# Scan of a Mamba-2 layer: two weightings written as scaled activations on ScalarE instead of GpSimd tensor products

## Chip, core and metric
One core of a Trainium2 chip runs the whole layer as one program. The metric is device time in microseconds (us), the median of the runs. The engines are named as the profile names them: PE (TensorE, matmul), DVE (VectorE), ACT (ScalarE), POOL (GpSimd), SP (SyncE, which here only issues DMAs).

## The reference, cut to what matters
```python
mod = (sc @ ada_w[i] + ada_b[i]).reshape(-1, 6, D_MODEL)      # sc = silu(c), D_MODEL = 1024
...
acum = jnp.cumsum(ac, axis=-1)                                # ac = dt * a, chunks of 128 tokens
scores = jnp.einsum("bclhn,bcshn->bhcls", ch, bh) * segsum_exp(ac)
y_diag = jnp.einsum("bclhs,bcshp->bclhp", scores, xdt)        # xdt = xs * dt
...
y_off = jnp.einsum("bclhn,bchpn,bhcl->bclhp", ch, states[:, :-1], jnp.exp(acum))
```
The modulation is a row vector (1024) times a matrix (1024 x 6144). The scan runs over 8 chunks of 128 tokens with 8 heads, forwards and backwards, with time steps `dt` for each token, head and direction. After it come an output projection, a selection of experts and their evaluation, which take most of the time and are not touched.

## The kernel before
The work around the change has three stretches. The **projection** (about 77 to 355 us) multiplies the tokens with 21 weight blocks on PE, with convolutions on DVE. The **backward loop** (about 355 to 433 us) has 12 steps `n` over `pre`: four for the context tokens, then the chunks 7 to 0. The **forward loop** (about 433 to 541 us) goes over the chunks 0 to 7. Each engine works through its own queue in the order in which the code issues instructions; SP issues the DMAs in such a queue too.

The modulation is computed in 24 slices beside the other work. A slice is a 512 KB block of `ada_w`, loaded by `ask()` (L293) into the tile `ld`, of which there are two buffers. `modulation()` multiplies it with `sc` (L320), one factor for each partition and each of 8 groups of 128 columns; DVE sums the 8 groups (L322, L323, L325), PE sums over partitions (L304). `beside()` runs a piece of this at the end of each loop step: first the sums of one slice, then the multiplication of the next. Six slices are multiplied in the projection, 12 in the backward loop, six in the forward loop.

`spread(z)` of the scan makes for a chunk the two tiles `pf` and `pb` (128 x 8 x 128): a triangular mask times `dt`, one factor for each partition and head (L648). `decays(z)` multiplies them on PE (L693, L694), ACT takes the exponent into `em` (L696), and DVE works on it.

Also in the loops are the key products `step_keys` (PE L356, into the one PSUM buffer `pk`; ACT copies it out into `h2T`, L358; after every second one SP stores it to `m_dram`, L360, and loads the next `wqT` block, L342). A backward step holds one key product, a forward step of the chunks 0 to 4 holds four. `reach` puts `dtx` on ACT (L625), from which PE and then ACT make `de` (L632); `natural` copies `xn` and `bn` out of PSUM on ACT (L592, L596); `weigh` (`xw`, L602) and the product with `dcol` (L598) are on POOL.

Of the kernel before, what the change touches and what calls it, by code (L numbers as in the profile page):

```python
# [13 lines left out]
AF = mybir.ActivationFunctionType  # L14
OP = mybir.AluOpType
# [3 lines left out]
P = 128  # L19
D = 1024  # L20
KD = D // P
# [8 lines left out]
NH = 8  # L30
# [42 lines left out]
def layer_kernel(ctx, tc, A, dbg=None):  # L73
    nc = tc.nc
# [32 lines left out]
    sc = glob.tile([P, KD, 2], F32, name="sc")  # L107
# [19 lines left out]
    dt = mixp.tile([P, NZ, 16], F32, name="dt")  # L127
# [168 lines left out]
    def modulation():  # L296

        nc.sync.dma_start(gater, A["ada_b"][2048:3072].partition_broadcast(P))
        last = []

        def spread(j, wa):
            row, k = j // KD, j % KD
            pr = prs[:, j % 4]
            nc.tensor.matmul(pr, ones, wa, start=True, stop=True)  # L304
            if row == 0:
                g = gater[:, k * P:(k + 1) * P]
                nc.vector.tensor_tensor(g, pr, g, op=OP.add)
            else:
                nc.vector.scalar_tensor_tensor(wa, pr, 1.0, ident, op0=OP.mult, op1=OP.mult,
                                               accum_out=(b2c if row == 1 else s2c)[:, k:k + 1])  # L310

        prs = psL.tile([P, 4, P], F32, name="pc")
        for j in range(24):
            while j not in ready:
                yield -1
            while last and last[0][0] < call[0]:
                spread(*last.pop(0)[1:])
                yield 0.25
            w = ready[j]
            nc.gpsimd.tensor_tensor(w, w, sc[:, :, 0:1].to_broadcast([P, KD, P]), op=OP.mult)  # L320
            yield -1
            nc.vector.tensor_tensor(w[:, :4], w[:, :4], w[:, 4:], op=OP.add)  # L322
            nc.vector.tensor_tensor(w[:, :2], w[:, :2], w[:, 2:4], op=OP.add)  # L323
            wa = lpr.tile([P, P], F32, name="wa", bufs=3)
            nc.vector.tensor_tensor(wa, w[:, 0], w[:, 1], op=OP.add)  # L325
            del ready[j]
            last.append((call[0], j, wa))
            yield 1.1
        yield -1
        while last:  # L330
            spread(*last.pop(0)[1:])
        nc.vector.tensor_tensor(b2c, b2c, adab[:, 24:32], op=OP.add)
        nc.vector.tensor_tensor(s2c, s2c, adab[:, 32:40], op=OP.add)
        nc.vector.tensor_scalar(s2c, s2c, 1.0, None, op0=OP.add)
        nc.vector.tensor_tensor(s2c, s2c, n2c, op=OP.mult)
        yield 1.0
# [30 lines left out]
    with ExitStack() as st:  # L367
# [123 lines left out]

        held = {}
        later.append(modulation())
        for n, c in enumerate(order):

# [80 lines left out]
    with ExitStack() as st:  # L576
# [67 lines left out]
        def spread(z):  # L644
            pf = s2p.tile([P, NH, P], F32, name="pf")
            pb = s2p.tile([P, NH, P], F32, name="pb", bufs=1)
            for d, (buf, half) in enumerate(((pf, upper), (pb, lower))):
                nc.gpsimd.tensor_tensor(buf, half[:, None].to_broadcast([P, NH, P]),  # L648
                                        dt[:, z, d * 8:d * 8 + 8, None].to_broadcast([P, NH, P]), op=OP.mult)
            C[z] = pf, pb  # L650

        pre = [(NT, 0), (NT + 1, 1), (NT + 1, 0), (NT, 1)] + [(z, 1) for z in range(NT - 1, -1, -1)]
# [6 lines left out]
        for n, (z, d) in enumerate(pre):  # L659
            nxt, far = None, iter(())  # L660
            if n + 1 < len(pre):
                zn = pre[n + 1][0]
                if zn in todo:
                    todo.remove(zn)
                    far = reach(zn, 1)
                    next(far)
                    natural(zn)
                if zn:
                    nxt = weigh(*pre[n + 1])
                if n == len(pre) - 4:  # L670
                    spread(0)
            step_keys(1)
            if z < NT:
                carried(z, 1, hs[1])
            if z:
                hs[d] = state(z, d, hs[d], xw)
            next(far, None)
            xw = nxt
            if n == 2:
                dbg("hf", hs[0])  # L680
            if n == 3:
                dbg("hb", hs[1])
            for q in range(2 * n, min(16, 2 * n + 2)):
                nc.vector.tensor_scalar(ltA[:, q], gt_s if q < 8 else lt_s, an[:, q:q + 1], None, op0=OP.mult)
            ask()
            beside(2.2)
# [928 lines left out]
```

## Time and profile before
| | us |
|---|---|
| median of 3 runs | 3078.5 |
| lowest and highest | 3078.39, 3080.2 |
| the profiled execution, its own time | 3079.81 |
| its span in the trace | 3078.1 |

Over the span PE is busy 92%, DVE 85%, POOL 44% and ACT 34%. These are averages over stretches with different limits; the scan has to be read by its own rows. In a row, busy time is followed by a count (x...), "idle before" names what ended a wait, and times in a timeline count from the span's start.

### The profile page before, as it was taken

What the parts mean: (1) busy time and instruction counts of PE and PEld (TensorE: products, weight loads), DVE (VectorE), ACT (ScalarE), POOL (GpSimd) and SP (SyncE); (2) the same over time, 40 slices, a digit from 0 to 9 for tenths busy, and PEclk for the clock granted to TensorE, in tenths of its full rate; (3) what the DMA queues carried; (4) which work ended last, traced back from release to release, by engine and by line L of the source; (5) the groups of instructions that cost most, each with busy time, mean ns of one, the idle gap of its engine ahead of it and who ended that gap; (6) DMA issues with size and microseconds to landing.
All of it is one profiled execution on the core that took longest, in us unless ns stands there. A gap on an engine that the chain in (4) does not pass through costs nothing.

```text
span 3078.1 us, 41667 instructions
## 1 busy us (share of the span) xinstructions
PE 2824.7 (92%) x14905; PEld 2374.3 (77%) x14905; DVE 2624.8 (85%) x5164; ACT 1061.4 (34%) x2026; POOL 1350.1 (44%) x1059
## 2 busy tenths in 40 slices
PE   7999878898888886999999999999999999999996
PEld 3777667664555556898888997998998898998894
DVE  4898788558999998889988888888988888888886
ACT  3224332332677664232322222222222322222222
POOL 0212455420000001666566666556666566666650
PEclk8999999899999987999999999999999999999998
DMA  6111346241212225898989998999998999999982
GB/s 212 61 35 48 100 141 192 83 160 56 117 66 103 110 110 190 303 315 312 314 307 329 336 345 316 325 350 324 335 338 315 327 344 325 338 330 334 321 314 108
DMA packets 334544, 722.66 MB, mean 235 GB/s; under 512 B 24560, under 2 KB 167168, under 8 KB 333056
## 3 DMA queue, kind: packets, MB, share of 16 engines
q0 software_dynamic: 112176, 408.47, 37.3%
q1 hardware_dynamic: 222160, 311.53, 28.9%
q8 instruction: 117, 1.92, 0.2%
q14 instruction: 91, 0.75, 0.1%
HBM read 658.56 MB, written 61.35 MB: 234 GB/s over the span
## 4 chain that ended last, share of the span: by engine, by line
PE 51%; DVE 30%; DMA 8%; issue 6%; POOL 4%; ACT 2%; SPq 0%; DVEq 0%; POOLq 0%; ACTq 0%
PE pa L990 22%; PE pv L1428 7%; PE pv L1429 7%; PE pv L1427 7%; DMA gr<-in_peer_u_dram,idx 4%; DVE o L1211 3%; DVE cfm L408 3%; PE pa L68 3%; DMA gr<-in_peer_v_dram,idx 2%; DVE oh L1083 2%; DVE ob L1203 2%; DVE gr L1299 2%; DVE oh L1081 2%; POOL gr L1276 2%; PE po L68 1%
## 5 line engine op out<-in xcount | busy, mean ns | idle before, releaser
L1276 POOL DMA_INDIRECT gr<-in_peer_u_dram,idx x384 | 524.8, 1367 | 370.3 <-DVE gr L1299 271.9
L1276 POOL DMA_INDIRECT gr<-in_peer_v_dram,idx x384 | 543.5, 1415 | 326.1 <-DVE h2T L1311 233.1
L1311 DVE SCALAR_TENSOR_TENSOR h2T<-gr,wv,h2T 128x1024 f32<-128x1024 f32 x381 | 488.5, 1282 | 47.5 <-DMA gr<-in_peer_v_dram,idx 41.1
L1428 PE MATMUL pv<-vl,wh 128*128 128x512 f32 x1240 | 496.0, 400 | 30.5 <-DVE vl L61 30.3
L1299 DVE SCALAR_TENSOR_TENSOR gr<-gr,h2T 128x1024 f32<-128x1024 f32 x384 | 458.1, 1221 | 51.0 <-DMA gr<-in_peer_u_dram,idx 50.3
L1427 PE MATMUL pv<-vh,wl 128*128 128x512 f32 x1240 | 493.4, 398 | 5.1 <-ACT vh L60 5.1
L1429 PE MATMUL pv<-vh,wh 128*128 128x512 f32 x1240 | 493.6, 398 | 0.0
L60 ACT ACTIVATE vh<-v 128x512 fp32r<-128x512 f32 x256 | 161.3, 632 | 666.6 <-PE pv L1429 636.3
L990 PE MATMUL pa<-hh,ul 128*128 128x320 f32 x2000 | 334.1, 309 | 0.7 <-DVE ul L982 0.7
L990 PE MATMUL pa<-hl,uh 128*128 128x320 f32 x2000 | 334.1, 309 | 0.3 <-ACT ga L1390 0.3
L990 PE MATMUL pa<-hh,uh 128*128 128x320 f32 x2000 | 334.0, 309 | 0.0
L990 PEld LDWEIGHTS pa<-hl,uh 128*128 128x128 f32 x2000 | 304.8, 188 | 3.5 <-ACT ga L1390 0.8
L1428 PEld LDWEIGHTS pv<-vl,wh 128*128 128x128 f32 x1240 | 236.3, 191 | 91.8 <-DVE vl L61 38.3
L990 PEld LDWEIGHTS pa<-hh,ul 128*128 128x128 f32 x2000 | 303.5, 188 | 1.2 <-DVE ul L982 1.2
L990 PEld LDWEIGHTS pa<-hh,uh 128*128 128x128 f32 x2000 | 303.6, 188 | 0.0
L1390 ACT ACTIVATE ga<-pa 128x320 f32<-128x320 f32 x252 | 109.6, 437 | 508.4 <-PE pa L990 507.4
L1427 PEld LDWEIGHTS pv<-vh,wl 128*128 128x128 f32 x1240 | 236.3, 191 | 60.7 <-ACT vh L60 6.4
L1429 PEld LDWEIGHTS pv<-vh,wh 128*128 128x128 f32 x1240 | 236.4, 191 | 54.5
L1189 PEld LDWEIGHTS pg<-o,o 128*128 128x128 f32 x1280 | 175.4, 208 | 126.8 <-ACT o L1206 106.6
L1189 PE MATMUL pg<-o,o 128*128 128x128 f32 x1280 | 189.5, 298 | 74.0 <-ACT o L1206 64.5
L61 DVE TENSOR_TENSOR vl<-v,vh 128x512 fp32r<-128x512 f32 x256 | 176.2, 689 | 95.1 <-ACT vh L60 94.7
L1206 ACT ACTIVATE o<-ob,tr 128x128 f32<-128x128 bf16 x640 | 209.3, 398 | 96.3 <-DVE ob L1203 94.3
(344 smaller groups left out, 4292.8 us busy)
## 6 DMA issues: line engine op xcount, KB each, us to landing
v<-in_peer_v_dram SPq DMA_DIRECT2D x256, 256.0 KB
u<-in_peer_ut_dram SPq DMA_DIRECT2D x87, 512.0 KB
g_dram<-stg SPq DMA_DIRECT2D x10, 4096.0 KB
gm<-g_dram SPq DMA_DIRECT2D x64, 640.0 KB
h2T<-in_peer_ut_dram SPq DMA_DIRECT2D x41, 512.0 KB
ld<-in_ada_w_dram SPq DMA_DIRECT2D x24, 512.0 KB
w<-in_w_in_t_dram SPq DMA_DIRECT2D x21, 512.0 KB
raw<-in_ada_w_dram SPq DMA_DIRECT2D x8, 1024.0 KB
```

Of the source, the lines that this page charges most:

```text
L60: nc.scalar.activation(hi, src, AF.Copy)
L61: (eng or nc.vector).tensor_tensor(lo, src, hi.bitcast(F32), op=OP.subtract)
L68: nc.tensor.matmul(out, a(k)[i], b(k)[j], start=start and t == 0 and k == 0, stop=stop and t == 2 and k == n - 1)
L990: nc.tensor.matmul(pa[half], x[:, k], y[:, k, half * TH:half * TH + TH], start=t == 0 and k == 0, stop=t == 2 and k == KD - 1)
L1189: nc.tensor.matmul(pg[:, j], o2[:, j], o1[:, j], start=True, stop=True)
L1206: nc.scalar.activation(o2[:, j], ob[:, :, j], AF.Copy, scale=tr[:, 1, t4 * 4 + j:t4 * 4 + j + 1])
L1276: nc.gpsimd.indirect_dma_start(out=g, out_offset=None, in_=A[t], in_offset=bass.IndirectOffsetOnAxis(ap=idx[:, b, e:e + 1], axis=0))
L1299: nc.vector.scalar_tensor_tensor(g, g, 1.0, h2, op0=OP.mult, op1=OP.mult, accum_out=act[:, e:e + 1])
L1311: nc.vector.scalar_tensor_tensor(ac, g, wv[:, e:e + 1], ac, op0=OP.mult, op1=OP.add)
L1427: nc.tensor.matmul(Out.pv[t], wl[:, sl], self.vh, start=i == 0, stop=False)
L1428: nc.tensor.matmul(Out.pv[t], wh[:, sl], self.vl, start=False, stop=False)
L1429: nc.tensor.matmul(Out.pv[t], wh[:, sl], self.vh, start=False, stop=i == GE - 1)
```

## The change
The multiplication of a slice, one GpSimd tensor product over 128 x 1024, becomes eight ScalarE activations (Copy with a scale for each partition) over 128 x 128, in place. `spread` becomes 16 such activations instead of two GpSimd products. Nothing else is edited.
```diff
             w = ready[j]
-            nc.gpsimd.tensor_tensor(w, w, sc[:, :, 0:1].to_broadcast([P, KD, P]), op=OP.mult)
+            for k in range(KD):
+                nc.scalar.activation(w[:, k], w[:, k], AF.Copy, scale=sc[:, k, 0:1])
             yield -1
...
             for d, (buf, half) in enumerate(((pf, upper), (pb, lower))):
-                nc.gpsimd.tensor_tensor(buf, half[:, None].to_broadcast([P, NH, P]),
-                                        dt[:, z, d * 8:d * 8 + 8, None].to_broadcast([P, NH, P]), op=OP.mult)
+                for h in range(NH):
+                    nc.scalar.activation(buf[:, h], half, AF.Copy, scale=dt[:, z, d * 8 + h:d * 8 + h + 1])
             C[z] = pf, pb
```
The lines behind the first place move down by one in the changed kernel, so that L358 there is L359, and so on.

ACT's queue in the forward loop, from the exponent `em` of one chunk to that of the next, before (names in brackets are the semaphores that an instruction waits for; DMAHW is a DMA's):
```order
L696 ACTIVATE em<-psg 128x1024 [waits PE_49]
L358 ACTIVATE h2T<-pk 128x512 [waits DMAHW0_49,PE_49]
L358 ACTIVATE h2T<-pk 128x512 [waits PE_49]
L632 ACTIVATE de<-ps 128x512 [waits DVE_49,PE_49]
L358 ACTIVATE h2T<-pk 128x512 [waits DMAHW4_49,PE_49]
L358 ACTIVATE h2T<-pk 128x512 [waits PE_49]
L625 ACTIVATE dtx<-dta 128x512 [waits Activation_49]
L696 ACTIVATE em<-psg 128x1024 [waits DVE_49,PE_49]
```
The same place in the changed kernel:
```order
L697 ACTIVATE em<-psg 128x1024 [waits PE_49]
L359 ACTIVATE h2T<-pk 128x512 [waits DMAHW0_49,PE_49]
L359 ACTIVATE h2T<-pk 128x512 [waits PE_49]
L633 ACTIVATE de<-ps 128x512 [waits PE_49]
L359 ACTIVATE h2T<-pk 128x512 [waits DMAHW4_49,PE_49]
L650 ACTIVATE pf<-tri,dt 128x128 [waits DVE_49]
L650 ACTIVATE pf<-tri,dt 128x128 x7
L650 ACTIVATE pb<-tri,dt 128x128 [waits DVE_49]
L650 ACTIVATE pb<-tri,dt 128x128 x7
L359 ACTIVATE h2T<-pk 128x512 [waits PE_49]
L321 ACTIVATE ld<-ld,sc 128x128 [waits DMAHW2_49]
L321 ACTIVATE ld<-ld,sc 128x128 x7
```
Twenty-four instructions have come in between: the 16 of `spread` ahead of the step's last `h2T`, and the eight of the slice behind it, the first of which waits for the slice's DMA. `dtx` and the next `em` (L626, L697) follow them.

ACT's queue in a backward step, before (from `dtx` to the `dtx` of the step after):
```order
L625 ACTIVATE dtx<-dta 128x512 [waits Activation_49]
L592 ACTIVATE xn_2338<-pdg 128x512 [waits PE_49]
L596 ACTIVATE bn_2339<-pcb 128x256 [waits PE_49]
L358 ACTIVATE h2T<-pk 128x512 [waits DMAHW4_49,PE_49]
L632 ACTIVATE de<-psg 128x512 [waits DVE_49,PE_49]
```
The same step in the changed kernel:
```order
L626 ACTIVATE dtx<-dta 128x512 [waits Activation_49]
L593 ACTIVATE xn_2415<-pdg 128x512 [waits PE_49]
L597 ACTIVATE bn_2416<-pcb 128x256 [waits PE_49]
L359 ACTIVATE h2T<-pk 128x512 [waits DMAHW4_49,PE_49]
L633 ACTIVATE de<-psg 128x512 [waits DVE_49,PE_49]
L321 ACTIVATE ld<-ld,sc 128x128 [waits DMAHW3_49,DVE_49,Activation_49]
L321 ACTIVATE ld<-ld,sc 128x128 x7
```
Here the slice stands behind `de` and ahead of the next step's `dtx`.

SP's queue in the changed kernel, around the load of the slice that the first forward step multiplies (DMAHW2, as in the ACT rows):
```order
L361 DMA m_dram<-h2T 128x8x128 [waits DMAHW6_49,DMAHW0_49,Activation_49]
L343 DMA h2T<-in_wqT_dram 128x1024 [waits DMAHW7_49]
L344 DMA sk<-in_skT_dram 128x128 [waits DMAHW1_49,PE_49]
L361 DMA m_dram<-h2T 128x8x128 [waits DMAHW4_49,Activation_49]
L293 DMA ld<-in_ada_w_dram 128x8x128 [waits DMAHW2_49,DVE_49]
```
The order of SP's DMAs is the one of before; the load (L293) stands behind a store that waits for ACT, and that ACT instruction is the step's last `h2T` (L359).

## Rows read from the trace of the kernel before
**Rows 1.** Windows of the backward and forward loop: busy time by engine, clock, DMA share.
```profile
355.00:433.00 78.00, 54.76 (x378) 49.30 (x377) 69.45 (x105) 25.79 (x49) 46.54 (x32) 0.96 0.55 168
433.00:541.00 108.00, 88.42 (x725) 81.59 (x723) 85.86 (x108) 28.50 (x44) 54.51 (x28) 0.91 0.56 172
```
**Rows 2.** The lines L320 and L648: durations min/median/max in ns; waits.
```profile
L320 POOL TENSOR_TENSOR ld<-ld,sc x24: 1902/1906/3152, 90.9 to 525.7; 128x1024 f32<-128x1024 f32 x24
...
DMA ld<-in_ada_w_dram: 64.9, 15
...
L648 POOL TENSOR_TENSOR pf<-tri,dt x8: 1891/1898/2871, 408.6 to 516.7; 128x1024 f32<-128x1024 f32 x8
...
PE psg L694: 8.3, 6
```
**Rows 3.** Timeline of DVE and POOL, forward loop: start, us, what.
```profile
453.61 0.69 DVE L617 TENSOR_TENSOR htmp<-h,tot 128x512 f32<-128x512 f32 x1
466.87 2.38 DVE L617 TENSOR_TENSOR htmp<-h,tot 128x512 f32<-128x512 f32 x1
...
466.35 2.34 POOL L648 TENSOR_TENSOR pb<-tri,dt 128x1024 f32<-128x1024 f32 x1
```
**Rows 4.** Timeline of ACT, later stage: four activations with a scale per partition.
```profile
880.86 1.30 ACT L1206 ACTIVATE o<-ob,tr 128x128 f32<-128x128 bf16 x4
```
**Rows 5.** Timeline of ACT, backward loop.
```profile
373.61 0.62 ACT L625 ACTIVATE dtx<-dta 128x512 f32<-128x512 f32 x1
...
374.87 0.61 ACT L358 ACTIVATE h2T<-pk 128x512 f32<-128x512 f32 x1
...
386.06 0.62 ACT L625 ACTIVATE dtx<-dta 128x512 f32<-128x512 f32 x1
...
400.49 0.62 ACT L625 ACTIVATE dtx<-dta 128x512 f32<-128x512 f32 x1
```
**Rows 6.** Timeline of SP and POOL, backward loop: a slice's issue and multiplication.
```profile
386.84 0.38 SPq L293 DMA_DIRECT2D ld<-in_ada_w_dram  x1
...
390.76 1.90 POOL L320 TENSOR_TENSOR ld<-ld,sc 128x1024 f32<-128x1024 f32 x1 [3.08 <-DMA ld<-in_ada_w_dram]
...
430.25 1.90 POOL L320 TENSOR_TENSOR ld<-ld,sc 128x1024 f32<-128x1024 f32 x1 [5.03 <-DMA ld<-in_ada_w_dram]
```
**Rows 7.** Timeline of ACT, forward loop.
```profile
433.07 1.03 ACT L696 ACTIVATE em<-psg 128x1024 f32<-128x1024 f32 x1 [5.95 <-PE psg L694]
...
447.04 1.02 ACT L696 ACTIVATE em<-psg 128x1024 f32<-128x1024 f32 x1 [10.62 <-PE psg L694]
...
458.82 1.02 ACT L696 ACTIVATE em<-psg 128x1024 f32<-128x1024 f32 x1 [2.68 <-PE psg L694]
459.74 0.59 ACT L358 ACTIVATE h2T<-pk 128x512 f32<-128x512 f32 x1
...
464.95 0.60 ACT L358 ACTIVATE h2T<-pk 128x512 f32<-128x512 f32 x1 [1.19 <-PE pk L356]
466.80 0.60 ACT L358 ACTIVATE h2T<-pk 128x512 f32<-128x512 f32 x1 [1.25 <-PE pk L356]
467.29 0.62 ACT L625 ACTIVATE dtx<-dta 128x512 f32<-128x512 f32 x1
...
526.45 1.02 ACT L696 ACTIVATE em<-psg 128x1024 f32<-128x1024 f32 x1 [11.40 <-PE psg L694]
```
**Rows 8.** Timeline of SP, POOL and PE in the same forward step.
```profile
467.42 0.38 SPq L360 DMA_DIRECT2D m_dram<-h2T  x1
467.90 0.52 SPq L293 DMA_DIRECT2D ld<-in_ada_w_dram  x1
...
473.34 1.90 POOL L320 TENSOR_TENSOR ld<-ld,sc 128x1024 f32<-128x1024 f32 x1 [4.65 <-DMA ld<-in_ada_w_dram]
...
461.07 1.16 PE L356 MATMUL pk<-sk,h2T 128*128 128x128 f32 x8
```
**Rows 9.** Windows at the first forward step, columns as in rows 1.
```profile
440.00:442.00 2.00, 0.85 (x4) 0.85 (x5) 0.67 (x1) 0.00 (x0) 2.00 (x2) 0.50 0.34 123
442.00:444.00 2.00, 2.00 (x11) 2.00 (x11) 0.00 (x0) 0.00 (x0) 1.96 (x2) 0.50 0.00 0
446.00:448.00 2.00, 2.00 (x21) 2.00 (x20) 1.11 (x1) 0.96 (x2) 0.00 (x0) 1.00 0.04 8
```

## The prediction
> **What bounds the kernel now.** I went from the page's chain of waits, where PE and DVE carry most of the span, to the windows of the stretches that the change touches. In the backward loop DVE is busy 69.45 of 78 us and PE 54.76; in the forward loop PE 88.42 of 108 and DVE 85.86; ACT has only 25.79 and 28.50 [rows 1]. So the engine that gets the work looks empty, and the engines it may relieve look full. What decides is therefore not ACT's busy share but where in its queue the new instructions stand, and what they wait for. For that I read the lines L320 and L648 with their waits, and then the timelines of ACT, SP, POOL and PE over single loop steps.
>
> The view of the lines says that POOL's 24 slice products take 1.91 us each and that 15 of them came after 64.9 us of waiting for the slice's DMA; the products of `spread` take 1.9 us or more each, and PE waited 8.3 us for them at L694 [rows 2]. The first is the important one: POOL stands still for slices, and today little stands behind it.
>
> The timelines also show DVE and POOL in each other's way. The same DVE product takes 0.69 us alone and 2.38 us when it starts 0.52 us after a POOL product of 2.34 us [rows 3].
>
> **The change part by part.** *Removed:* 24 slice products and 16 spread products on POOL, 24 x 1.91 + 16 x 1.90 = 76 us by the medians [rows 2], and DVE's stretching beside them. The sum of DVE's stretching is worth nothing where another engine sets the step; its size is weighed under the rivals.
>
> *The price of one new activation* is not in the trace for this shape and these types. The nearest row has four activations over 128 x 128 with a per-partition scale in 1.30 us [rows 4]: taking 0.40 for the last and 0.30 from start to start for the three others, 0.30 x 3 + 0.40 = 1.30. A slice of eight is then 7 x 0.30 + 0.40 = 2.5 us and holds the next instruction up by 2.4; a spread of 16 holds it up by 4.8. These stand on ACT, in order. If the pitch were 0.35, a step with both would cost 24 x 0.05 = 1.2 us more.
>
> *Projection.* Six slices, 6 x 2.4 = 14 us of ACT, lie beside PE's matmuls, whose evictions have three PSUM buffers. I price this at 0. If the cover is gone, it is the last two slices, ahead of two evictions that feed DVE: up to 2 x 2.4 = 5 us. On the other side DVE has some 2 us of stretching less. Bounds -2 and +5.
>
> *Backward loop.* A slice's load is issued when DVE has summed the one before it, and lands 390.76 - 386.84 = 3.9 us later [rows 6]. Behind the slice ACT now holds `dtx`, `xn`, `bn`, `h2T` and `de` of the next step; from `dtx`'s start to `h2T`'s end they take 374.87 + 0.61 - 373.61 = 1.9 us back to back [rows 5], with `de` 2.4. In every second step SP has a store of `m_dram` ahead of the load, and that store waits for `h2T`. There the loop is: slice ends, 1.9 to the end of `h2T`, 0.5 for SP's store, 5.4 to the landing (the forward price below), 2.5 for the next slice: 10.3 us. In the step after it the load goes out earlier, in the shade of this, so: 2.4 + 2.4 = 4.8. A pair is 15.1, where two steps now take 400.49 - 386.06 = 14.4 [rows 5]: +0.7 for each of some four pairs, +3. The spread of chunk 0 stands in ACT's queue too, 4.8, where its POOL version cost about 3 more in its step: +2. The last slice is waited for once more and its 2.5 and the `dtx` behind it precede the first `em`, which today follows 433.07 - 432.15 = 0.9 after POOL's slice at 430.25 ends [rows 6, 7]: +3.5. So the first `em` is some 9 us late. From there to the second `em` the rows have 447.04 - 433.07 = 14.0 [rows 7], lengthened by POOL's spread and a half clock; on ACT it is about 0.9 + 1.0 for `de` and `h2T`, 2.8 until the first `pb` piece, 5 for PE's decay products: 10. The second `em` is late by 9 - 4 = 5, bounds -5 and +10.
>
> *Forward loop,* the main term. Five steps (chunks 0 to 4) have this queue on ACT: `em`, `h2T`, `h2T`, `de`, `h2T`, 16 of spread, `h2T`, eight of the slice, `dtx`, `em`. The load of the slice stands in SP's queue behind the store that waits for the last `h2T`; in the trace that store is issued at 467.42, as `h2T` of 466.80 ends, the load at 467.90, and POOL starts at 473.34 [rows 7, 8]. So a slice cannot be there before 0.02 + 0.48 + 5.44 = 5.9 us after that `h2T` ends. POOL bears this wait today with little behind it. ACT will stand in it with the next chunk's `dtx`, `em` and `h2T`, and PE's second key product needs the one PSUM buffer that this `h2T` empties. The queued cycle, from the start of that key product (461.07 [rows 8]):
> to the third `h2T` 464.95 - 461.07 = 3.9 [rows 7, 8]; its pitch 0.5; spread 4.8; the last `h2T` 0.6; store, load and landing 5.9; slice 2.4; `dtx` 0.5 (467.29 - 466.80 shows such a pitch); `em` 459.74 - 458.82 = 0.9; `h2T` 0.6 and 0.05 to PE [rows 7]. Sum 20.2 us.
> Within it PE can run ahead by its decay products, one key product and the products of the chunk before, then has nothing for about 7 us. Where PE had been busy only 0.85 of 2 us, the clock stood at 0.50 (1.2 GHz); it still did in the next 2 us, all busy, and was at 1.00 (2.4 GHz) from 446 to 448 [rows 9]. I add 2 us, half of the 3.9 at the low level: 22.2. Bounds 18.7 (a landing in 3.9 and no clock loss) and 25 (all 3.9 doubled, 1.2 for pitch).
> The last interval, chunk 5, has no key products; I take 13 (ACT's chain with one more wait for a slice; bounds 11 and 18). Now the six intervals take 526.45 - 447.04 = 79.4 [rows 7]. After: 5 x 22.2 + 13 = 124. That is +45, bounds 5 x 18.7 + 11 = 104.5, +25, and 5 x 25 + 18 = 143, +64.
>
> *Sum:* 0 + 5 + 45 = +50. Behind the scan nothing takes it back: the output projection begins with `y` of the last chunk. The profiled execution took 3079.81, 1.7 over its span and 1.3 over the median; on the median the forecast is 3078.5 + 50 = **3128**. Corners of all bounds at once (+18 and +79) are rarer than one; for this case I take +26 to +66.
>
> **A rule beside the rows.** A row pair shows DVE waiting out a POOL product, 1.7 us in one instruction [rows 3]. The Trainium skill, GPSIMD Engine Reference, section 1 (Specifications), says that GpSimd's SBUF interfaces are shared with VectorE and contend with its instructions with two SBUF inputs; the pair agrees. By the rule alone DVE's steps get shorter and the time falls, as in the first rival below; by the queues it rises.
>
> **The rivals.**
> *Faster: DVE and POOL are untangled and ACT's waits hide.* For it: the stretched DVE row [rows 3], DVE's 69.45 of 78 [rows 1], ACT's idle share. Then the forward steps fall to PE's own 458.82 - 447.04 = 11.8, 6 x 11.8 = 71 instead of 79.4, -9; the first interval falls by 2; the backward steps fall from 7.2 to some 6, -10: 3078.5 - 21 = 3057. It decides if the slice has landed when ACT comes to it, and if ACT's own 14.3 us a step (20.2 - 5.9) hid as well; I see nothing that would. Chance 0.05.
> *ACT's work counts, the wait for the slice does not.* If loads ran a step ahead, the forward cycle would be 14.3: 5 x 14.3 + 13 = 84.5, +5, and with the backward loop about +8: 3086. Against it: the store and the load in SP's queue [rows 8]. Chance 0.08.
> *PE's clock stays low through the scan.* Each forward cycle then pays the upper bound, and the backward steps some 1 to 2 more: 5 x 25 + 13 = 138, +59, and +15: 3152. For it: the windows at 0.50 [rows 9]; against: PE still works 11.8 of 22 us. Chance 0.08.
> *Nothing:* the scan's delay is absorbed and 3078 stays. PE waits for nothing but this chain there. Chance 0.03.
>
> **How the numbers follow.** My case has 0.76 and the time 3128, its own range 3104 to 3144. The range to hold 8 in 10 takes in the second rival and part of the clock rival: 3084 to 3150. A measurement of this kernel can tell about 0.2%, 6 us, from no change. Faster holds the first rival and a little of mine gone wrong, 0.06; the same 0.04; slower 0.90.
>
> **What would show it.** In the changed profile: L321 on ACT in eights of about 2.5 us, with some 6 us of idle time ahead of each in the forward loop, ended by the DMA of `ld`; intervals of 20 to 24 us between `em` rows; PE waiting for ACT at the key products (L357); DVE's L618 at 0.7 us nearly everywhere and the scan still longer, by 40 to 55 us; the stretches before 355 us and behind the scan unchanged. I would be wrong if the load were issued ahead of the store, if the slice landed much sooner than 5.4 us after its issue, or if the activations had another pitch than 0.30.

## The result, and the profile after

The changed kernel takes 3144.43 us (median of four runs, 3140.9 to 3157.01); the kernel before, run beside it, 3079.35 (3078.39 to 3085.02). The ratio is 1.0218, 95% interval 1.0202 to 1.0235: 65 us slower. The forecast was 3128 (3084 to 3150). The profiled execution took 3140.9 us, with a span of 3139.1.

The scan has all of it. Its eight exponents `em` serve as a clock below: the first is at 456.89 us (before 433.07), the second at 469.46 (447.04), the last at 591.27 (526.45). So the backward side costs 23.8 us, the first interval gives 1.4 back, and the rest of the forward loop costs 42.4. The load of `nw`, the first behind the scan, is issued at 603.01 instead of 540.40, which is 62.6 later, and the profiled execution takes 61.1 us more than the one before: the stretches behind the scan give back only a few us.

Windows of the loops, columns as in [rows 1]. The stretches are the same times of the span; the work in them is less, since the loops last longer.
```profile
355.00:433.00 78.00, 51.83 (x290) 47.05 (x289) 42.70 (x89) 46.21 (x127) 17.93 (x17) 0.80 0.42 122
433.00:541.00 108.00, 73.05 (x530) 68.78 (x529) 47.03 (x73) 59.21 (x161) 7.75 (x7) 0.83 0.43 125
```
ACT, the engine that got the work, is busy 59.21 of 108 us; DVE has fallen to 47.03 and PE to 73.05. No engine is full. That is how a chain of waits looks, and the view of waits from 355 to 610 us names it (us in total, times, longest):
```profile
ACT ld L321 <- DMA ld<-in_ada_w_dram: 63.4, 13, 6.3
...
PE pk L357 <- ACT h2T L359: 33.0, 6, 7.2
...
PE psg L630 <- ACT dtx L626: 19.6, 4, 5.6
```
ACT stands for slices, and PE stands for what is queued behind them. POOL did the same before [rows 2], with less in its queue (what stood there shows in e8). The lines of the two new groups over the whole span (count, then busy us and mean ns, then idle time ahead and its releasers):
```profile
L321 ACT ACTIVATE ld<-ld,sc 128x128 f32<-128x128 f32 x192 | 58.6, 388 | 71.9 <-DMA ld<-in_ada_w_dram 71.6 <-DVE ld L323 0.3
...
L650 ACT ACTIVATE pb<-tri,dt 128x128 f32<-128x128 f32 x64 | 19.5, 390 | 0.0
```
One forward step on ACT, from `em` to `em` (compare [rows 7]):
```profile
489.99 1.00 ACT L697 ACTIVATE em<-psg 128x1024 f32<-128x1024 f32 x1
490.89 0.58 ACT L359 ACTIVATE h2T<-pk 128x512 f32<-128x512 f32 x1
493.64 0.60 ACT L359 ACTIVATE h2T<-pk 128x512 f32<-128x512 f32 x1 [2.17 <-PE pk L357]
495.07 0.60 ACT L633 ACTIVATE de<-ps 128x512 f32<-128x512 f32 x1 [0.84 <-PE ps L630]
496.86 0.60 ACT L359 ACTIVATE h2T<-pk 128x512 f32<-128x512 f32 x1 [1.19 <-PE pk L357]
497.35 2.44 ACT L650 ACTIVATE pf<-tri,dt 128x128 f32<-128x128 f32 x8
499.69 2.43 ACT L650 ACTIVATE pb<-tri,dt 128x128 f32<-128x128 f32 x8
502.03 0.58 ACT L359 ACTIVATE h2T<-pk 128x512 f32<-128x512 f32 x1
508.42 2.44 ACT L321 ACTIVATE ld<-ld,sc 128x128 f32<-128x128 f32 x8 [5.82 <-DMA ld<-in_ada_w_dram]
510.77 0.61 ACT L626 ACTIVATE dtx<-dta 128x512 f32<-128x512 f32 x1
511.29 1.00 ACT L697 ACTIVATE em<-psg 128x1024 f32<-128x1024 f32 x1
```
and on SP (the rows of before are in [rows 8]):
```profile
502.63 0.38 SPq L361 DMA_DIRECT2D m_dram<-h2T  x1
503.10 0.53 SPq L293 DMA_DIRECT2D ld<-in_ada_w_dram  x1
```
The last `h2T` ends at 502.61; 0.02 later the store goes out, 0.47 later the slice's load, and 5.32 later ACT can start on the slice. PE in the same step:
```profile
491.52 2.08 PE L357 MATMUL pk<-sk,h2T 128*128 128x128 f32 x8 [6.68 <-ACT h2T L359]
493.39 1.64 PE L630 MATMUL ps<-tri,dtx 128*128 128x128 f32 x8
494.87 1.06 PE L640 MATMUL ps<-CT,h 128*128 128x128 f32 x8
...
503.36 0.39 PE L695 MATMUL psg<-pb,ltA 128*128 128x128 f32 x2
```
PE had finished the input of `em` soon after 503.36; `em` ran at 511.29, because it stands behind the slice. An engine that takes its queue in order cannot step over an instruction whose data are late. (The Trainium skill, Perfetto Trace Analysis, section "Tensor Engine Instruction (MATMUL, LD_WEIGHTS)", calls ACT, DVE and GpSimd strict FIFO; these rows agree.)

### The profile page after: what moved, and what is told of

Read it like the earlier page. It is cut to its first block, busy times and chain, and to the rows that moved or that the text cites. A ratio compares the mean times of both kernels' runs of the same rounds, so it can differ in the third digit from the quotient of the medians.

```text
span 3139.1 us, 41947 instructions
## 1 busy us (share of the span) xinstructions
PE 2842.5 (91%) x14905; PEld 2394.4 (76%) x14905; DVE 2582.1 (82%) x5164; ACT 1151.2 (37%) x2346; POOL 1260.6 (40%) x1019
## 4 chain that ended last, share of the span: by engine, by line
PE 47%; DVE 31%; DMA 8%; issue 5%; ACT 5%; POOL 3%; SPq 1%; DVEq 0%; POOLq 0%; ACTq 0%
PE pa L991 19%; PE pv L1429 7%; PE pv L1430 7%; PE pv L1428 7%; DVE o L1212 3%; DVE cfm L409 3%; DMA gr<-in_peer_u_dram,idx 3%; DVE gr L1300 2%; DMA ld<-in_ada_w_dram 2%; POOL gr L1277 2%; DVE oh L1084 2%; DVE ob L1204 2%; DVE cfm L411 2%; DVE oh L1082 2%; DVE ef L1070 1%
```

## The experiments

Theory (queue): ACT stands in the slice's transfer, with `dtx`, `em` and `h2T` behind it. Rival 1 (work): what costs is the time of the activations themselves. Rival 2 (clock): what costs is PE's lower clock. The table has the exponents' times from each profile, the mean of the five intervals from the second exponent to the seventh ("step"), the median, and the ratio to the kernel before on the same chip (whose median was 3081.57 for e1 to e4, 3079.11 for e5 to e8 and 3077.49 for e9).

| | first `em` | second | last | step | median | ratio, interval |
|---|---|---|---|---|---|---|
| before | 433.07 | 447.04 | 526.45 | 12.9 | 3079.35 | |
| changed | 456.89 | 469.46 | 591.27 | 21.8 | 3144.43 | 1.0218 (1.0202 to 1.0235) |
| e1 spread only | 430.43 | 440.98 | 529.97 | 14.5 | 3081.97 | 0.9999 (0.9982 to 1.0015) |
| e2 slices only | 454.72 | 463.87 | 571.34 | 19.0 | 3125.37 | 1.0136 (1.0112 to 1.016) |
| e3 changed, early load | 433.76 | 446.56 | 529.55 | 14.7 | 3080.92 | 1.0003 (0.9989 to 1.0018) |
| e4 e1, early load | 430.44 | 441.23 | 524.48 | 14.8 | 3079.57 | 0.9997 (0.998 to 1.0013) |
| e5 one piece of eight | 435.31 | 447.23 | 538.80 | 15.8 | 3098.04 | 1.0065 (1.0042 to 1.0089) |
| e6 load ahead of one store | 433.46 | 446.30 | 536.88 | 14.5 | 3092.87 | 1.0045 (1.0031 to 1.006) |
| e7 before, early load | 433.85 | 447.43 | 515.96 | 12.1 | 3075.63 | 0.9976 (0.9962 to 0.9989) |
| e8 loops' slices, early load | 429.22 | 435.48 | 503.49 | 12.0 | 3055.78 | 0.9915 (0.9893 to 0.9937) |
| e9 all slices, early load | 433.03 | 440.91 | 508.02 | 11.8 | 3061.22 | 0.9949 (0.9933 to 0.9964) |

**e1: only `spread` on ACT.** The kernel before with the second hunk of the change.

> Only spread is on ScalarE (16 activations a chunk), the slices stay on GpSimd as before. Queue theory (the lost time is ScalarE standing in the slice's DMA wait): nothing on ScalarE waits for a transfer, its own work in a forward step is 0.9 + 4 x 0.6 + 0.6 + 4.8 + 0.5 = 9.2 us, under the steps of before; 3065 to 3090. Work theory (the activations' own time is what costs): 4.8 of the 7.2 us that each of five forward steps got are still there, so about two thirds of the forward loop's 42 us, 3105 to 3115. Clock theory (PE's lower clock is most of it): the clock in the forward loop returns to about 0.91 only if the steps do.

The time is that of before. The work rival falls as the cause of the 65 us: two thirds of the forward loop's added work are there and 65 us are not. But the step is not shorter than before either, 14.5 against 12.9.

**e2: only the slices on ACT.** The kernel before with the first hunk.

> Only the slices are on ScalarE, spread stays on GpSimd. Queue theory: the forward cycle loses 4.8 us of spread and keeps the wait, 20.3 measured mean - 4.8 = 16 to 17.5 us, 12 to 20 us over before for the loop, and the backward loop's +22 stays: 3110 to 3130. Work theory: only 2.4 of 7.2 us a forward step remain, 14 us in the forward loop and some 20 in the backward loop by their own time of 12 x 2.4 = 29 less cover: about 3095 to 3105, with the intervals between exponents under 15 us.

3125.37, inside the queue theory's range; the first exponent is 21.7 late, nearly as in the changed kernel. The step, 19.0, is longer than the 16 to 17.5 expected. ACT in the step from 500.85 to 519.47:
```profile
507.65 0.60 ACT L359 ACTIVATE h2T<-pk 128x512 f32<-128x512 f32 x1 [1.19 <-PE pk L357]
509.50 0.60 ACT L359 ACTIVATE h2T<-pk 128x512 f32<-128x512 f32 x1 [1.25 <-PE pk L357]
516.60 2.45 ACT L321 ACTIVATE ld<-ld,sc 128x128 f32<-128x128 f32 x8 [6.50 <-DMA ld<-in_ada_w_dram]
```
The last `h2T` comes 1.85 after the third, held by PE's key product; with `spread` between them it came 502.03 - 496.86 = 5.2 after. So leaving `spread` out shortens the chain by 3.3, not 4.8, and the slice's wait is longer.

**e3: the changed kernel, its load a step earlier.** No instruction is added; `ask()` goes to the step's start. It does the same in the backward loop.
```diff
         for z in range(NT):
+            ask()
             more = z + 1 < NT
...
             step_keys(1)
-            ask()
             beside(2.2)
```

> The changed kernel, with the slice's load issued at the start of a loop step instead of its end, so that it has a step's time to land and stands ahead of the store in SP's queue. No instruction is added or taken away. Queue theory: the waits of about 6 us ahead of L322 in the forward loop vanish, the cycle falls from 22 to about 14.3 us, the backward pairs from 17 to 14 or 15: 3080 to 3105. Work theory and clock theory: ScalarE does the same work, so 3130 to 3145.

3080.92: with all the added work still on ACT, the whole loss is gone. ACT's wait for slices from 355 to 610 us, and the windows of the forward loop:
```profile
ACT ld L321 <- DMA ld<-in_ada_w_dram: 13.0, 8, 5.8
```
```profile
433.00:541.00 108.00, 88.23 (x724) 80.72 (x724) 65.16 (x97) 74.70 (x207) 5.21 (x5) 0.95 0.56 172
```
and the end of a step on ACT:
```profile
487.63 0.57 ACT L359 ACTIVATE h2T<-pk 128x512 f32<-128x512 f32 x1
488.11 2.43 ACT L321 ACTIVATE ld<-ld,sc 128x128 f32<-128x128 f32 x8
490.44 0.61 ACT L626 ACTIVATE dtx<-dta 128x512 f32<-128x512 f32 x1
490.96 1.00 ACT L697 ACTIVATE em<-psg 128x1024 f32<-128x1024 f32 x1
```
The slice follows `h2T` without a gap. The granted clock is 0.95 (0.83 in the changed kernel), though nothing was done for it: rival 2 is a consequence of the wait, not a cause beside it.

**e4: e1 with the early load**, the edit of e3 made to e1.

> Spread on ScalarE, slices on GpSimd, and the load issued at the start of a loop step. Queue theory: 3055 to 3085, under the kernel before if what GpSimd waited for its slices had anything behind it (the first exponent of the forward loop followed such a slice by 0.9 us). Work theory: 3105 to 3115, as with spread alone.

3079.57, in the range but without a gain, and its step is e3's. So the slices on ACT cost nothing in e3's step, and it is `spread` in ACT's queue that keeps it at 14.7.

**e5: the wait almost without the work.** The kernel before; one of a slice's eight pieces is an activation.
```diff
-            nc.gpsimd.tensor_tensor(w, w, sc[:, :, 0:1].to_broadcast([P, KD, P]), op=OP.mult)
+            nc.scalar.activation(w[:, 0], w[:, 0], AF.Copy, scale=sc[:, 0, 0:1])
+            nc.gpsimd.tensor_tensor(w[:, 1:], w[:, 1:], sc[:, 1:, 0:1].to_broadcast([P, KD - 1, P]), op=OP.mult)
```

> The kernel before, in which of each slice's eight pieces one is an activation on ScalarE and seven stay on GpSimd; spread stays on GpSimd. ScalarE gets 24 x 0.39 = 9 us of work in all, but stands in every slice's DMA wait. Queue theory: each loop step costs what slices alone on ScalarE cost (forward steps 19.3, first exponent 21.7 late) less 7 x 0.29 = 2.1 a step: forward steps about 17, first exponent 12 to 17 late, 3098 to 3120. Work theory: 9 us of work spread over 464 us, 3078 to 3085.

3098.04, the lower edge of the queue theory's range, and well above the 3085 of the work rival: 9 us of work, put where it waits, cost 19 (13 to 27 by the interval). The profile is of the fastest of its four executions; in it the last exponent is 12 us later than before, and the execution is 12 us longer. The wait from 355 to 610 us, and one forward step's, on ACT:
```profile
ACT ld L320 <- DMA ld<-in_ada_w_dram: 84.5, 17, 10.0
```
```profile
469.96 0.60 ACT L359 ACTIVATE h2T<-pk 128x512 f32<-128x512 f32 x1 [1.25 <-PE pk L357]
477.02 0.40 ACT L320 ACTIVATE ld<-ld,sc 128x128 f32<-128x128 f32 x1 [6.47 <-DMA ld<-in_ada_w_dram]
```
Two parts of the expectation were wrong: the step, 15.8, is under the 17 expected, and the backward loop makes the first exponent 2.2 late, not 12 to 17. By the pair worked out in the prediction, 15.1 with two slices of 2.5, two of 0.4 make 15.1 - 4.2 = 10.9, under the 14.4 that the pair takes anyway [rows 5]; I had subtracted from the loss instead of working out the pair. ACT stands longer here than in the changed kernel (84.5 against 63.4 us), and it costs less than a third.

**e6: how early is early.** The changed kernel with `ask()` ahead of a step's last key product (in both loops), past one store only.
```diff
                 hf = state(z, 0, hf, xw)
+            ask()
             step_keys(1)
-            ask()
             beside(2.2)
```

> The changed kernel, with the slice's load moved ahead of the last key product of a loop step, so that only its place against the store of m_dram in SP's queue changes by one. In the forward loop it then goes out some 8 us sooner (after the step's middle store instead of the last). If the store that waits for ScalarE is what makes the load late: no wait at L321 in the forward loop, steps of 14.5 to 15 us, 3078 to 3095. If the slice needs a whole step's lead: waits of 3 us and more stay, steps over 17, 3105 to 3125.

3092.87. In the five steps with key products the wait is 1.2 us at most and the step 14.5, as in e3: passing that one store is enough. In chunk 5, without key products, the load went out at 523.78 and ACT could start at 534.01, 10.2 later. The last interval is 17.9, in e3 9.4, and at the last exponent 7 of the 12 us over e3 are there; the rest arises behind the scan, where I have not followed it.
```profile
516.15 2.43 ACT L321 ACTIVATE ld<-ld,sc 128x128 f32<-128x128 f32 x8
...
534.01 2.44 ACT L321 ACTIVATE ld<-ld,sc 128x128 f32<-128x128 f32 x8 [8.39 <-DMA ld<-in_ada_w_dram]
```
SP shows what stood ahead of that load, eight loads of `w_out` of 512 KB each:
```profile
516.69 6.00 SPq L365 DMA_DIRECT2D h2T<-in_w_out_dram  x8
523.78 0.38 SPq L293 DMA_DIRECT2D ld<-in_ada_w_dram  x1
```
From 520 to 532 us the DMA engines' share is 1.01 to 1.02. In e3 the slice's load goes out ahead of the eight (517.88, the eight from 519.96), and ACT does not wait for it. The changed kernel and the one before have the order of e6: their last slice's load is issued at 577.86 and 515.12, and the slice is multiplied 10.5 us later (588.39 and 525.66). Their longer last intervals (13.0 and 15.1) go with this order, though no run changes it alone.

**e7: the kernel before with the early load.**

> The kernel before, nothing on ScalarE, with the slice's load issued at the start of a loop step. GpSimd waited 65 us for 15 slices, but little stands behind it: 3070 to 3080. If GpSimd's waits bounded the loops, the backward steps of 7.2 us fall to about 6 and the time to 3060 or under.

3075.63, a little faster. The last exponent is 10.5 us earlier, so the late load did cost something in the kernel before: 0.8 a forward step, and the last interval is 8.2 instead of 15.1. Of the 10.5, 10.0 are left at the load of `nw` (530.35) and 3.5 in the median. The rest is lost behind the scan, where I have not followed it.

**e8: the version that the experiments point to.** e7 with the loops' slices on ACT; `spread` and the projection's slices stay on POOL.
```diff
+            if j < 6:
                 nc.gpsimd.tensor_tensor(w, w, sc[:, :, 0:1].to_broadcast([P, KD, P]), op=OP.mult)
+            else:
+                for k in range(KD):
+                    nc.scalar.activation(w[:, k], w[:, k], AF.Copy, scale=sc[:, k, 0:1])
```

> The slices of the two loops on ScalarE, those of the projection and all of spread on GpSimd, the load issued at the start of a loop step. It keeps what e3 gained (backward steps shorter with DVE no longer stretched by GpSimd's slices) and leaves out what cost there: 4.6 us at the end of the projection, and spread's 4.8 us a step in ScalarE's queue (forward steps 14.7, before 13.2). Theory: first exponent 5 to 8 earlier than before, forward steps 12.5 to 13.5: 3062 to 3074. If ScalarE's slices cost by themselves 2.4 us a step: 3085 to 3100.

3055.78, faster than both kernels by more than I expected (ratio to before 0.9915). A step on ACT (its lines stand three further down than in the changed kernel):
```profile
467.91 0.60 ACT L362 ACTIVATE h2T<-pk 128x512 f32<-128x512 f32 x1 [1.25 <-PE pk L360]
468.41 2.44 ACT L324 ACTIVATE ld<-ld,sc 128x128 f32<-128x128 f32 x8
470.75 0.61 ACT L629 ACTIVATE dtx<-dta 128x512 f32<-128x512 f32 x1
471.71 1.02 ACT L700 ACTIVATE em<-psg 128x1024 f32<-128x1024 f32 x1 [0.35 <-PE psg L698]
```
Slice, `dtx` and `em` follow at once, and `em` waits for PE again. Four of the five intervals are 11.8, which the prediction worked out as PE's own time. Against e7 the first exponent is 4.6 earlier and the first interval 6.3 instead of 13.6; these two make 12.0 of the 12.5 us at the last exponent, so the gain over e7 does not come from the steps. The interval is the place where something important stood behind the slices on POOL: in the kernel before, two slice products (430.25, after 5.03 of waiting for the DMA, and 433.43) stand ahead of chunk 1's `spread`, and PE waits for its `pb` (2.35 us; 3.68 in e7). In e8 that `pb` (second row) starts 9.5 us sooner than before (first row):
```profile
438.23 2.87 POOL L648 TENSOR_TENSOR pb<-tri,dt 128x1024 f32<-128x1024 f32 x1
428.73 1.90 POOL L652 TENSOR_TENSOR pb<-tri,dt 128x1024 f32<-128x1024 f32 x1 [12.51 <-DVE pf L701]
```

**e9: e8 with the projection's slices on ACT too**, that is e3 with `spread` back on POOL.

> All 24 slices on ScalarE with the load issued at the start of a loop step, spread on GpSimd: it differs from e3 by spread alone, from e8 by the projection's six slices alone. If spread in ScalarE's queue is what keeps e3 at the time of before (forward steps 14.6 against 11.8 in e8): forward steps of 11.8 to 12 here, 3052 to 3064, some 20 under e3. If what e8 won over e3 came from the projection instead: forward steps of 14 to 15 and 3070 to 3080. The projection's slices delay the first backward step by 4 to 5 us; as e3 made these good by the first exponent only in part, I expect 2 to 5 over e8.

3061.22, steps of 11.8. Against e3, taking `spread` out of ACT's queue is worth 20 us (17 by the two ratios): 3 a step, and 12.8 - 7.9 = 4.9 in the first interval. That is its price where the slices are on ACT as well; with the slices on POOL, e4 (`spread` alone on ACT) is only 4 us over e7 (6.5 by the ratios; 8.5 at the last exponent). Against e8, the projection's slices on ACT make the first exponent 3.8 later.

## Why the prediction came out as it did

The forecast had the second exponent 5 late and the last one 45 more; they were 22.4 and 42.4. The time, 3144.43, lies just above the range given to that case alone (3104 to 3144). It is inside 3084 to 3150 because that range was widened for part of the clock rival, which is not what happened: that much is luck.

**Where the loss arises and how** was right: ACT standing in the slice's transfer, behind a store that waits for ACT's own last `h2T`. e3 and e6 show it by moving the load alone.

**The forward loop** was priced at +45 from the second exponent to the last, and measured +42.4. The cycle, term by term from the rows of the changed kernel, from the key product at 491.52: to the third `h2T` 5.3 (3.9 at the high clock), its pitch 0.5, spread 4.7 (4.8), `h2T` 0.6, store, load and landing 5.8 (5.9), slice 2.35 (2.4), `dtx` 0.5, `em` 0.9, `h2T` and PE's start 0.6; together 21.3, against 20.2 and 2 for the clock. The last interval was 13.0, as forecast.

**The clock's term** was 2 and is 1.5. Windows of the same step:
```profile
486.00:488.00 2.00, 0.00 (x0) 0.00 (x0) 0.00 (x0) 0.88 (x3) 0.00 (x0) 0.95 0.88 324
488.00:490.00 2.00, 0.00 (x0) 0.00 (x0) 0.00 (x0) 2.00 (x8) 0.00 (x0) 0.50 0.01 5
490.00:492.00 2.00, 0.48 (x2) 0.48 (x3) 0.98 (x1) 1.47 (x3) 0.00 (x0) 0.50 0.00 0
492.00:494.00 2.00, 2.00 (x11) 2.00 (x11) 1.90 (x3) 0.36 (x1) 0.00 (x0) 0.50 0.00 0
```
PE has nothing from 486 to 490, the clock falls to 0.50 (1.2 GHz), and the key product takes 2.08 instead of 1.16 [rows 8] and L630 1.64 instead of the 1.06 of the like product L640 behind it: 0.9 + 0.6. Over five steps some 7 of the 42 us.

**The price of an activation** held: 388 ns, and 2.35 from a slice's start to `dtx`, 0.294 a piece (0.30 from [rows 4]). The Trainium skill, ScalarE: Activation LUTs, section "What ACT_TABLE_LOAD costs", gives a time per column, a surcharge for an operand that is a pointer, and an overlap back to back; an estimate from them for 128 columns is 386 ns for one and 293 from start to start, and the trace agrees (388 and 294).

**The backward side is the term that was mis-sized:** the second exponent was to be 5 late (-5 to +10) and is 22.4 late. By PE's key products it splits so: step n = 1 (the first that has one) starts 5.2 late (364.98, before 359.74), step 4 14.1 late (387.76, before 373.63), step 11 21.3 late (446.26, before 424.91), the first exponent 23.8. Steps 1 and 4, before and changed:
```profile
359.74 1.13 PE L356 MATMUL pk<-sk,h2T 128*128 128x128 f32 x8 [1.14 <-DMA sk<-in_skT_dram]
373.63 1.06 PE L356 MATMUL pk<-sk,h2T 128*128 128x128 f32 x8
...
364.98 1.06 PE L357 MATMUL pk<-sk,h2T 128*128 128x128 f32 x8
387.76 1.56 PE L357 MATMUL pk<-sk,h2T 128*128 128x128 f32 x8
```
- The projection was priced at 0 and costs 5.2, the upper bound. A slice in ACT's queue holds up the eviction behind it: ACT is 1.6 late ahead of the slice at 250.74 and 4.0 late behind it (L537 runs at 253.08, before at 249.12). Most of the 5.2 is there long before the last two slices, where the prediction looked for it; another slice holds up L506 at the end. "Beside PE's matmuls" was no cover for an eviction.
- The context steps were left out. I counted pairs of chunk steps, but slices are waited for in the first steps too:
```profile
372.49 2.44 ACT L321 ACTIVATE ld<-ld,sc 128x128 f32<-128x128 f32 x8 [4.47 <-DMA ld<-in_ada_w_dram]
374.84 0.57 ACT L359 ACTIVATE h2T<-pk 128x512 f32<-128x512 f32 x1
...
381.17 2.44 ACT L321 ACTIVATE ld<-ld,sc 128x128 f32<-128x128 f32 x8 [5.76 <-DMA ld<-in_ada_w_dram]
383.52 0.61 ACT L626 ACTIVATE dtx<-dta 128x512 f32<-128x512 f32 x1
```
  and PE stands behind them:
```profile
375.46 2.08 PE L357 MATMUL pk<-sk,h2T 128*128 128x128 f32 x8 [3.10 <-ACT h2T L359]
...
384.19 2.08 PE L630 MATMUL psg<-tri,dtx 128*128 128x128 f32 x8 [5.21 <-ACT dtx L626]
```
  They cost 14.1 - 5.2 = 8.9.
- The rest was near: the steps from 4 to 11 cost 7.2 where +0.7 a pair and 2 for `spread` made about 5 (`dtx` at 389.50, 405.23 and 422.57: pairs of 15.7 and 17.3, forecast 15.1), the end 2.5 (3.5). The 0.9 us from POOL's slice to the first `em`, which the prediction used there, is no dependence: `em` starts at 433.07 as PE's last decay product ends (432.65 + 0.39 = 433.04), and the early load moves it neither in e7 (433.85) nor in e4 (430.44, e1 430.43). The first interval gave back 1.4, not 4.

**The rivals.** "ACT's work counts, the wait does not" is e3: a cycle of 14.7 (forecast 14.3) and 3080.92 (3086). "Faster" named its two conditions, the slice landed and ACT's work hidden: e3 meets the first alone and gains nothing, e8, which keeps `spread` off ACT, both and takes 3055.78 (3057). The parts agree less than the sum: at the last exponent e8 has 3.9 from the backward side, 7.7 from the first interval and 11.4 behind it, where 10, 2 and 9 were worked out. The untangling of DVE and POOL is not what pays in the forward steps: DVE's L618 is 0.69 us long there in the changed kernel (2.38 before [rows 3]) while the step grows by 9 us, and in e7 that product still takes 1.53 with a step within 0.1 us of e8's. What the Trainium skill, GPSIMD Engine Reference, section 1 (Specifications), says of the SBUF interfaces shared with GpSimd bears on that instruction's length; by these runs it does not set the length of the step.

**What I had not seen** is that wait and work don't add. With the wait and little work (e5) the step is 2.9 longer than before and the first exponent 2.2 later; with the work and little wait (e3) 1.9 and 0.7; with both 8.9 and 23.8. For the slices alone the step says the same: +2.9 with the wait and an eighth of the work (e5), -1.1 with the work and no wait (e9), +6.1 with both (e2). I read this as: either alone fits mostly into ACT's idle time; both, one behind the other in one queue, don't.

Left open: what makes e8's first exponent 4.6 earlier than e7's, and what the stretches behind the scan make of earlier and later ends. At the load of `nw` e7 is 10.0 ahead and keeps 3.5 in the median; e8 is 24.5 ahead, and keeps 23 in the median but 15.7 in its profiled execution, the slowest of its four; e5 is 10.9 behind and loses 19 in the median.

## What to carry to other kernels

Before work is moved to an engine that looks idle, look at what its first instruction will wait for, and at what stands behind it in the new queue: a wait that was nearly free on the old engine is paid by everything queued there. If that wait is a transfer, look where the load stands in the issuing queue and what the DMAs ahead of it wait for; here the load stood behind a store that waited for the very engine that got the work, and moving the load's call in both loops was worth the whole loss. Then try the parts of the change apart and together: with the load early, the loops' slices on ACT gained 20 us (e8 against e7), and `spread` on ACT as well lost 20 (e3 against e9).

## What was unexpected

One activation of 0.40 us a slice, put where ACT waits 6 us for its data, costs 19 us in the median (e5): about as much as the 16 activations of `spread` a chunk that wait for no transfer (e3 against e9, 20 us). The same 512 KB load took 5.3 us from its issue to ACT's start in the changed kernel's step and 10.2 in e6's last, where it stood behind the eight loads of `w_out`. And the clock's fall, which looks large in the windows (0.83 of the forward loop, before 0.91), is worth only some 7 us and goes with the wait.
